# A hybrid decoder trunk on one core: two norms' reciprocals spread by split fp32r products, and conformer's variance computed in halves

## The chip, the cores and the metric

The kernel runs on one core of a Trainium2 chip. Five engines of the core work side by side, each through its own list of instructions in order: TensorE (PE in the profile, with its weight loads shown as PEld), VectorE (DVE), ScalarE (ACT), GpSimd (POOL) and SyncE (SP), which here only issues DMA. The metric is device time in microseconds of one execution, the median over several runs.

## The reference

One decoder layer on a sequence of 256 positions with 2048 features: an RMS norm, one wide input projection, sparse attention beside a causal conformer convolution, a shared output projection with a residual, a second RMS norm, a gated MLP with a short convolution, and a last RMS norm. The change touches the layer norm inside the conformer and the second RMS norm:

```python
def rms_norm(x, g):
    xf = x.astype(jnp.float32)
    y = xf * lax.rsqrt(jnp.mean(xf * xf, axis=-1, keepdims=True) + NORM_EPS)
    return (y * g.astype(jnp.float32)).astype(x.dtype)

def layer_norm(x, g, b):
    xf = x.astype(jnp.float32)
    mu = jnp.mean(xf, axis=-1, keepdims=True)
    xc = xf - mu
    var = jnp.mean(xc * xc, axis=-1, keepdims=True)
    y = xc * lax.rsqrt(var + NORM_EPS) * g.astype(jnp.float32) + b.astype(jnp.float32)
    return y.astype(x.dtype)
...
    u = layer_norm(u, ln_g, ln_b)
    return jax.nn.silu(u)
...
        x = x + jnp.concatenate([attn, conv], axis=-1) @ w_out[l]
        h = rms_norm(x, ffn_norm_g[l])
        x = x + conv_glu_ffn(h, w_up[l], ffn_conv_w[l], ffn_conv_b[l], w_down[l])
```

## The kernel before, in words

**Layout.** Activations lie feature by feature: 128 features on the partitions, 256 positions along the row. The weights come as tiles of 128x2048 fp32 (`wraw`, 1 MB each) over SyncE's queue. Each is split in two fp32r parts: ScalarE writes the high part `wh` (L126), VectorE or GpSimd the rest `wl = wraw - wh` (L131). The activations are split in the same way. A product is then three or so fast fp32r products with the high and low parts, summed in PSUM: the main stream is L454/L456 in the input projection, L189 to L191 in the output projection, L1188/L1190 in the MLP's first projection. Tiles are split two ahead of their use, out of three buffers.

**Order.** TensorE's list is written by hand. Between the products of a tile a `hook` (L428) runs at fixed places: it takes one step each from the lists `conf` (the conformer) and `steps`, and so many ticks of the attention (`attn_tick`, L980) as a table says. A tick does a slice of each of several stages (scores, smallest value, exponential, transposes, values) of different heads. The values of a head pair (`st_out`, L955) are products of 64 weight columns each, two halves `r` in turn, into the two halves of PSUM bank 7 (L966, L969). The last values' group is in the last tick, in the third tile of the output projection.

**Spreading a per-position number.** Both norms need one factor for each position in every partition. The sum over the features arrives with the positions on the partitions. GpSimd raises it to the power -0.5, VectorE multiplies the identity matrix `ident` by that column, which makes a 128x128 diagonal for each half `t` of the positions, and a product with a matrix of `ones` as weights writes that diagonal's values into all partitions. In the conformer that is `conf_var` (L578, the sum of the squares into two columns of bank 6), `conf_rstd` (L599), `conf_diag` (L606) and `conf_spread` (L584, then ScalarE copies the bank to `ck`), one per hook, started by `conf_norm` (L633) when the output projection's tile n = 2 begins. In the second norm it is `x2_rstd` (L1090) for each `t` and `x2_spread` (L1094) into bank 4, then a copy to `rB`; `x2_spread` is put by the table `between` (L1172) behind product pair 8 of the second half of the MLP's first tile, while the last feature blocks are still being transposed and split ahead of it (L1058, L225, L226). `rB` is applied only when the MLP's first results are taken out of PSUM, so TensorE's main stream does not wait for it.

`ones` and the diagonals are fp32 here, so these products run as fp32 products, and TensorE's list takes two passes for each.

Of the kernel before, what the change touches and what calls it, by code (L numbers as in the profile page):

```python
# [11 lines left out]
F32 = mybir.dt.float32  # L12
F32R = mybir.dt.float32r
AF = mybir.ActivationFunctionType
OP = mybir.AluOpType
PSUM = bass.MemoryType.PSUM

P = 128
T = 256
# [31 lines left out]
def hybrid_trunk(ctx: ExitStack, tc: tile.TileContext, a: dict, out: bass.AP):  # L51
    nc = tc.nc
# [148 lines left out]

    ident = consts.tile([P, P], F32, name="ident")
    make_identity(nc, ident)
    ones = consts.tile([P, P], F32, name="ones")
    nc.vector.memset(ones, 1.0)
    half = consts.tile([P, 1], F32, name="half")
    nc.vector.memset(half, -0.5)
# [10 lines left out]
    def rstd_of(pool, parts_, count, acc=EPS):  # L218

        r = pool.tile([P, 1], F32, name="rstd", bufs=2)  # L220
        nc.gpsimd.tensor_tensor(r, mean_of(pool, parts_, count, acc), half, op=OP.pow)
        return r

    def norm_evac(src, k, g):
        nc.scalar.activation(xt_h[:, k], src, AF.Copy, scale=g[:, k:k + 1])  # L225
# [11 lines left out]
    with ExitStack() as mx:  # L237
# [340 lines left out]
        def conf_var():  # L578
            cf["b"] = bank[6][:, :T]
            for t in range(2):  # L580
                nc.tensor.matmul(cf["b"][:, t:t + 1], cf["s"][:, 0, t * P:(t + 1) * P], ones[:, :1],
                                 start=True, stop=True)

        def conf_spread():  # L584
            nc.tensor.matmul(cf["b"], ones, cf["d"].rearrange("p t c -> p (t c)"), start=True, stop=True)
            conf_keep()

        def conf_apply(op, j0, n=2):
# [15 lines left out]
            cf["r"] = rv  # L604

        def conf_diag():  # L606
            cf["d"] = wk.tile([P, 2, P], F32, name="dg", tag="sg")
            for t in range(2):
                nc.vector.tensor_scalar_mul(cf["d"][:, t], ident, cf["r"][:, t:t + 1])

        def conf_swish(j0):
            for j in range(j0, j0 + 4):
# [19 lines left out]

        def conf_norm():  # L633
            conf.extend((
                no, no, conf_var, no, conf_rstd, no, conf_diag, no, conf_spread, no,
                *[lambda j=j: conf_apply(OP.mult, j) for j in (0, 2, 4, 6)],
                lambda: conf_swish(0), lambda: conf_swish(4), lambda: conf_split(0), lambda: conf_split(4)))

# [248 lines left out]


        TR_BANKS = (3, 6)
        units = [(i, r, br) for i in range(8) for r in range(2) for br in range(2)]  # L890
        US = {}

# [62 lines left out]
        def st_out(n):  # L955
            i = n // 4
            if n % 4 < 3:
                return
            o, q, m = bank[7], i // 4, i // 2
            assert cbst["done"] > m  # L960
            kw = dict(skip_group_check=True)
            for br in range(2):
                es = [US.pop(4 * i + 2 * r + br) for r in range(2)]
                for b, cols in enumerate((slice(0, T), slice(P, T))):
                    for r in range(2):
                        nc.tensor.matmul(o[64 * r:64 * r + 64, cols], vt[:, b, br, q, r],  # L966
                                         es[r][:, :T] if b == 0 else es[r][:, T:], start=br + b == 0, stop=False, **kw)
            for r in range(2):
                nc.tensor.matmul(o[64 * r:64 * r + 64, :T], vc[:, i % 2, q, r], cm["t"][:, m], start=False, stop=True,  # L969
                                 **kw)  # L970
            nc.scalar.activation(ma_h[:, i], o[:, :T], AF.Copy)
            nc.vector.tensor_sub(ma_l[:, i], o[:, :T], ma_h[:, i].bitcast(F32))
# [89 lines left out]
            norm_evac(x2_at(k), k, ffn_g)  # L1062

        for n, (qr, g) in enumerate(OUT_ORDER):
            if n == 1:
                assert tick["n"] > NU - 2
            if n == 2:
                x2 = mixp.tile([P, 2, D], F32, name="x2")
                nc.scalar.dma_start(ffn_g, a["vecs"][:, :KD])
                for t in range(2):  # L1070
                    nc.scalar.dma_start(x2[:, t], x_rows[:, t])
            if n == 2:
                conf_norm()
            if n == 3:
                assert tick["n"] == NU + DEEP
                st["lag"] = False
            if n == 8:
                step(count=99)
            ws = w_next(2)
            for t in range(2):  # L1080
                out_part(n, ws, qr, g, t)
                if g == 3:
                    steps.append(lambda qr=qr, t=t: out_resid(qr, t))
            if g == 3 and qr < 3:
                steps.extend([lambda: None] * 2 + [lambda qr=qr: (x2_tr(qr, 0), x2_tr(qr, 1))]
                             + [lambda k=k: (x2_evac(k), x2_evac(k + 1)) for k in range(4 * qr, 4 * qr + 4, 2)])
        acc = [mean_of(mixp, [ss2[:, t, i:i + 1] for i in range(3)], D) for t in range(2)]
        step(count=99)
        dg = mixp.tile([P, 2, P], F32, name="dg2")
        def x2_rstd(t):  # L1090
            r2 = rstd_of(mixp, [ss2[:, t, 3:4]], D, acc[t])
            nc.vector.tensor_scalar_mul(dg[:, t], ident, r2)

        def x2_spread():  # L1094

            for t in range(2):
                nc.tensor.matmul(bank[4][:, t * P:(t + 1) * P], ones, dg[:, t], start=True, stop=True)
            nc.scalar.activation(rB, bank[4][:, :T], AF.Copy)


    with ExitStack() as fx:
# [65 lines left out]
                    stages.remove(q)  # L1167


        for t in range(2):  # L1170
            x2_rstd(t)
        between = {(0, 6): lambda: (x2_tr(3, 0), x2_tr(3, 1)),  # L1172
# [207 lines left out]
```

## Time and profile before

| | |
|---|---|
| median of 3 runs | 1095.48 us (1095.45 to 1095.52) |
| the profiled execution's own time | 1095.29 us |
| its span, first to last instruction | 1093.5 us |
| granted TensorE clock, mean | 0.998 |
| TensorE busy | 1084.9 us, 99% |
| VectorE busy | 791.0 us, 72% |
| ScalarE busy | 602.2 us, 55% |
| GpSimd busy | 186.8 us, 17% |

The span lies inside the execution's time; what is around it (1.79 us) is start and end. A group row names line, engine, operation, what is written and read, the shape and the count, then busy time and mean ns. The chain of waits is followed back from the last instruction, and lists in order of time what the end depended on, with start and length in microseconds; on TensorE its lengths are the steps from one product to the next, while the durations in a timeline are modelled and overlap. In a timeline the bracket is the idle time ahead of an instruction and what ended it.

### The profile page before, as it was taken

How to read it: one execution, taken by the hardware profiler on the slowest of the kernel's cores; microseconds unless marked ns; L12 is line 12 of the kernel's file. 1: busy time of each engine (PE TensorE's matmuls, PEld its weight loads, DVE VectorE, ACT ScalarE, POOL GpSimd, SP SyncE). 2: the span in 40 equal slices, each digit the busy share in tenths (PEclk: the TensorE clock that was granted, in tenths of full speed). 3: DMA queues.
4: the chain of work that ended last, by engine and by line, in shares of the span. 5: the costliest groups of instructions: out<-in, count | busy, mean ns of one | idle time of the engine just before them, and what ended most of it. 6: DMA issues, size and time to landing. Idle time of an engine off the chain costs nothing.

```text
span 1093.5 us, 16270 instructions
## 1 busy us (share of the span) xinstructions
PE 1084.9 (99%) x6418; PEld 947.6 (87%) x6418; DVE 791.0 (72%) x1318; ACT 602.2 (55%) x915; POOL 186.8 (17%) x139
## 2 busy tenths in 40 slices
PE   9999999999999999999999999999999999999997
PEld 9888899887788888888888888888888888888886
DVE  7799989875656677777777777777777655665675
ACT  7644667887645555555555555545555544544552
POOL 0898775766000000000000000000000000000000
PEclk9999999999999999999999999999999999999999
DMA  9677535323654655555555555555554555556642
GB/s 363 241 265 261 178 127 174 116 78 138 248 193 166 237 186 192 191 190 192 193 192 193 193 188 186 187 186 186 189 191 151 193 188 189 198 179 203 232 161 77
DMA packets 34216, 207.55 MB, mean 190 GB/s; under 512 B 3883, under 2 KB 6715, under 8 KB 14428
## 3 DMA queue, kind: packets, MB, share of 16 engines
q1 hardware_dynamic: 30620, 199.46, 51.8%
q10 hardware_dynamic: 3520, 7.06, 1.8%
q8 instruction: 50, 0.82, 0.3%
q14 instruction: 26, 0.21, 0.1%
HBM read 204.39 MB, written 2.12 MB: 189 GB/s over the span
## 4 chain that ended last, share of the span: by engine, by line
PE 96%; DVE 2%; ACT 1%; issue 1%; POOLq 0%; POOL 0%; DVEq 0%; ACTq 0%
PE bank L1188 30%; PE bank L1207 17%; PE bank L1190 15%; PE bank L454 9%; PE bank L456 5%; PE bank L189 3%; PE bank L191 3%; PE bank L190 3%; PE bank L198 1%; PE bank L196 1%; PE bank L966 1%; PE bank L197 1%; PE bank L199 1%; PE bank L947 1%; PE bank L167 1%
## 5 line engine op out<-in xcount | busy, mean ns | idle before, releaser
L126 ACT ACTIVATE wh<-wraw 128x1024 fp32r<-128x1024 f32 (+3 forms) x248 | 355.8, 1452 | 344.5 <-issue 136.6
L131 DVE TENSOR_TENSOR wl<-wraw,wh 128x2048 fp32r<-128x2048 f32 (+2 forms) x194 | 361.7, 1873 | 206.1 <-ACT wh L126 206.1
L1188 PE MATMUL bank<-xt,wh 128*128 128x512 f32 x1408 | 488.5, 394 | 0.0
L1190 PE MATMUL bank<-xt,wl 128*128 128x256 f32 x1408 | 390.1, 277 | 0.0
L1188 PEld LDWEIGHTS bank<-xt,wh 128*128 128x128 f32 x1408 | 264.0, 188 | 61.2
L1190 PEld LDWEIGHTS bank<-xt,wl 128*128 128x128 f32 x1408 | 264.4, 188 | 0.0
L454 PE MATMUL bank<-xt,wh 128*128 128x512 f32 x464 | 150.6, 395 | 0.0
L1244 POOL TENSOR_TENSOR rstd<-ss,half 128x1 f32<-128x1 f32 x2 | 1.1, 548 | 730.4 <-DVE ss L1241 730.4
L131 POOL TENSOR_TENSOR wl<-wraw,wh 128x1024 fp32r<-128x1024 f32 (+1 forms) x54 | 121.2, 2271 | 19.8 <-ACT wh L126 15.3
L456 PE MATMUL bank<-xt,wl 128*128 128x256 f32 x464 | 105.8, 280 | 0.0
L489 DVE SCALAR_TENSOR_TENSOR bank<-us,cw,bank 128x256 f32<-128x256 f32 x232 | 95.0, 481 | 4.2 <-ACT bank L484 3.5
L454 PEld LDWEIGHTS bank<-xt,wh 128*128 128x128 f32 x464 | 80.8, 188 | 12.8 <-issue 0.6
L456 PEld LDWEIGHTS bank<-xt,wl 128*128 128x128 f32 x464 | 83.5, 188 | 8.4
L1207 PE MATMUL bank<-wl,gh 128*128 128x512 f32 x352 | 89.9, 336 | 0.0
L1207 PE MATMUL bank<-wh,gl 128*128 128x512 f32 x352 | 89.8, 336 | 0.0
L1207 PE MATMUL bank<-wh,gh 128*128 128x512 f32 x352 | 89.8, 336 | 0.0
L1151 DVE SCALAR_TENSOR_TENSOR yt<-u,fcw,yt 128x255 f32<-128x255 f32 (+1 forms) x176 | 80.9, 480 | 3.1
L941 POOL TENSOR_SCALAR e<-e,lsum 128x128 f32<-128x128 f32 x64 | 59.2, 940 | 36.3 <-ACT qs L824 15.7
L1207 PEld LDWEIGHTS bank<-wl,gh 128*128 128x128 f32 x352 | 54.1, 188 | 7.0
L1207 PEld LDWEIGHTS bank<-wh,gl 128*128 128x128 f32 x352 | 54.1, 188 | 6.9
L1207 PEld LDWEIGHTS bank<-wh,gh 128*128 128x128 f32 x352 | 54.0, 188 | 6.9
L1147 ACT ACTIVATE yt<-u,fcw 128x256 f32<-128x256 f32 x88 | 47.4, 586 | 0.0
(222 smaller groups left out, 1237.8 us busy)
## 6 DMA issues: line engine op xcount, KB each, us to landing
wraw<-in_w_u SPq DMA_DIRECT2D x88, 1024.0 KB, 4.8
wraw<-in_w_d SPq DMA_DIRECT2D x44, 768.0 KB, 4.2
wraw<-in_w_t SPq DMA_DIRECT2D x29, 1024.0 KB, 5.0
wraw<-in_w_o SPq DMA_DIRECT2D x16, 1024.0 KB, 5.0
wraw<-in_w_dl SPq DMA_DIRECT2D x11, 1024.0 KB, 4.8
wraw<-in_w_vg SPq DMA_DIRECT2D x4, 608.0 KB, 4.5
hb<-in_head SPq DMA_DIRECT2D x2, 1024.0 KB, 10.9
xr<-in_x SPq DMA_DIRECT2D x2, 1024.0 KB, 19.0
```

Of the source, the lines that this page charges most:

```text
L126: nc.scalar.activation(h[:, sl], raw[:, sl], AF.Copy)
L131: (nc.gpsimd if pooled else nc.vector).tensor_sub(l[:, sl], raw[:, sl], h[:, sl].bitcast(F32))
L189: nc.tensor.matmul(ps, xh, wh, start=first, stop=False)
L454: nc.tensor.matmul(ps, wh[:, sl], xt[:, kt].rearrange("p a t -> p (a t)"), start=kt == 0, stop=False)
L456: nc.tensor.matmul(ps[:, T:], wl[:, sl], xt_h[:, kt], start=False, stop=kt == KD - 1)
L489: nc.vector.scalar_tensor_tensor(y[:, j] if last else acc[0], us[:, j, k:k + T], cw[:, j, k:k + 1], acc[0], op0=OP.mult, op1=OP.add)
L941: nc.gpsimd.tensor_scalar_mul(e[:, lo:hi], e[:, lo:hi], lsum[:, br, t:t + 1])
L1147: nc.scalar.activation(yt, us_[i], AF.Identity, scale=fcw[:, c, 2:3], bias=fcw[:, c, 3:4])
L1151: nc.vector.scalar_tensor_tensor(ys[i][:, d:], us_[i][:, :T - d], fcw[:, c, k:k + 1], ys[i][:, d:], op0=OP.mult, op1=OP.add)
L1188: nc.tensor.matmul(bk[i], wh[:, k, sl], xt[:, kt].rearrange("p a t -> p (a t)"), start=kt == 0, stop=False)
L1190: nc.tensor.matmul(bk[i][:, T:], wl[:, k, sl], xt_h[:, kt], start=False, stop=kt == KD - 1)
L1207: nc.tensor.matmul(banks[n][:, :hi - lo], g[p][:, kt % 4, sl], ws[w][:, k * DW + lo:k * DW + hi], start=kt + i == 0, stop=i == 2 and kt == ...
```

## The change

Three things are changed.

1. `ones` becomes an fp32r tile (`ones_r`), with an fp32 view of the same bytes for all its other uses.
2. The diagonals of both norms are written in two fp32r parts by `diag_split`: the high part `identity * r`, and the rest `identity * r - high`. The spread is then two fp32r products of 256 columns with `ones_r`, summed in PSUM: in place of one fp32 product of 256 columns in the conformer, and of two with 128 in the second norm. The second norm's two tiles `dg2_h` and `dg2_l` lie in the MLP's pool `fp`, which takes over the memory of the pools of the mixer; `dg2` lay in `mixp`, the pool that lasts for the whole kernel.
3. `conf_var` makes its two products as four with 64 weight columns each, and is taken out of the conformer's list: it is put into the list `beside` when tile n = 2 begins, and `st_out` runs it ahead of the values of a whole group. The place is the last values' group.

```diff
-    ones = consts.tile([P, P], F32, name="ones")
+    ones_r = consts.tile([P, P], F32R, name="ones")
+    ones = ones_r.bitcast(F32)
...
+    def diag_split(d, t, r):
+        nc.vector.tensor_scalar_mul(d[0][:, t], ident, r)
+        nc.vector.scalar_tensor_tensor(d[1][:, t], ident, r, d[0][:, t].bitcast(F32), op0=OP.mult, op1=OP.subtract)
...
         def conf_var():
             cf["b"] = bank[6][:, :T]
             for t in range(2):
-                nc.tensor.matmul(cf["b"][:, t:t + 1], cf["s"][:, 0, t * P:(t + 1) * P], ones[:, :1],
-                                 start=True, stop=True)
+                for h in range(0, P, 64):
+                    nc.tensor.matmul(cf["b"][h:h + 64, t:t + 1], cf["s"][:, 0, t * P + h:t * P + h + 64], ones[:, :1],
+                                     start=True, stop=True)
 
         def conf_spread():
-            nc.tensor.matmul(cf["b"], ones, cf["d"].rearrange("p t c -> p (t c)"), start=True, stop=True)
+            for n, d in enumerate(cf["d"]):
+                nc.tensor.matmul(cf["b"], ones_r, d.rearrange("p t c -> p (t c)"), start=n == 0, stop=n == 1)
             conf_keep()
...
         def conf_diag():
-            cf["d"] = wk.tile([P, 2, P], F32, name="dg", tag="sg")
+            cf["d"] = [wk.tile([P, 2, P], F32R, name=nm, tag="sg") for nm in ("dg_h", "dg_l")]
             for t in range(2):
-                nc.vector.tensor_scalar_mul(cf["d"][:, t], ident, cf["r"][:, t:t + 1])
+                diag_split(cf["d"], t, cf["r"][:, t:t + 1])
...
-                no, no, conf_var, no, conf_rstd, no, conf_diag, no, conf_spread, no,
+                no, no, no, no, conf_rstd, no, conf_diag, no, conf_spread, no,
...
+        beside = []
...
             if n % 4 < 3:
                 return
+            while beside:
+                beside.pop(0)()
...
         for n, (qr, g) in enumerate(OUT_ORDER):
+            if n == 2:
+                beside.append(conf_var)
...
-        dg = mixp.tile([P, 2, P], F32, name="dg2")
         def x2_rstd(t):
             r2 = rstd_of(mixp, [ss2[:, t, 3:4]], D, acc[t])
-            nc.vector.tensor_scalar_mul(dg[:, t], ident, r2)
+            diag_split(dg, t, r2)
 
         def x2_spread():
 
-            for t in range(2):
-                nc.tensor.matmul(bank[4][:, t * P:(t + 1) * P], ones, dg[:, t], start=True, stop=True)
+            for n, d in enumerate(dg):
+                nc.tensor.matmul(bank[4][:, :T], ones_r, d.rearrange("p t c -> p (t c)"), start=n == 0, stop=n == 1)
             nc.scalar.activation(rB, bank[4][:, :T], AF.Copy)
...
+        dg = [fp.tile([P, 2, P], F32R, name=nm) for nm in ("dg2_h", "dg2_l")]
         for t in range(2):
             x2_rstd(t)
```

The order of instructions moves in three places. On TensorE, before, around conformer's variance in the third tile of the output projection (banks are numbered from 64 here, so bank_70 is bank 6 and bank_71 bank 7; `s` holds the folded squares, a shape is weight columns by columns):

```order
L581 MATMUL bank_70<-ones,s_2018 128x1 x2
L189 MATMUL bank_67<-wh,ma_h 128x512
L190 MATMUL bank_67<-wl,ma_h 128x512
L191 MATMUL bank_67<-wh,ma_l 128x512
L189 MATMUL bank_67<-wh,ma_h 128x512
L190 MATMUL bank_67<-wl,ma_h 128x512
L191 MATMUL bank_67<-wh,ma_l 128x512
L966 MATMUL bank_71<-es,vt 64x256 x2
L966 MATMUL bank_71<-es,vt 64x128 x2
```

And on TensorE after, at the same place (L587, L976 are the changed kernel's lines of the variance and the values):

```order
L189 MATMUL bank_67<-wh,ma_h 128x512
L190 MATMUL bank_67<-wl,ma_h 128x512
L191 MATMUL bank_67<-wh,ma_l 128x512
L587 MATMUL bank_70<-ones,s_2018 64x1 x4
L976 MATMUL bank_71<-es,vt 64x256 x2
L976 MATMUL bank_71<-es,vt 64x128 x2
```

The variance has moved behind six products of the main stream, and stands directly ahead of the values, with 64 weight columns as they have.

On VectorE, before, the diagonals of the second norm, at the start of the MLP, with the semaphores that an instruction waits for (`ms` is the mean of squares, `rstd` the reciprocal root, `dg_3710` the tile `dg2`, `x_3126` the residual stream):

```order
L1049 TENSOR_TENSOR x_3126<-bank_71,x_3126 128x512 [waits PE_49]
L214 TENSOR_SCALAR ms<-ss_2865,ms 128x1 [waits Activation_49]
L1092 TENSOR_SCALAR dg_3710<-ident,rstd 128x128 [waits Pool_49]
L214 TENSOR_SCALAR ms<-ss_2865,ms 128x1 [waits Activation_49]
L1092 TENSOR_SCALAR dg_3710<-ident,rstd 128x128 [waits Pool_49]
L226 SCALAR_TENSOR_TENSOR xt<-bank_64,ffn_g,xt 128x256 [waits Activation_49]
```

And after, where `dg_h` and `dg_l` are the two tiles' parts, and L231 is the old L226:

```order
L1059 TENSOR_TENSOR x_3126<-bank_71,x_3126 128x512 [waits PE_49]
L215 TENSOR_SCALAR ms<-ss_2865,ms 128x1 [waits Activation_49]
L226 TENSOR_SCALAR dg_h<-ident,rstd 128x128 [waits Activation_49,Pool_49]
L227 SCALAR_TENSOR_TENSOR dg_l<-ident,rstd,dg_h 128x128 [waits DVE_49]
L215 TENSOR_SCALAR ms<-ss_2865,ms 128x1
L226 TENSOR_SCALAR dg_h<-ident,rstd 128x128 [waits Pool_49]
L227 SCALAR_TENSOR_TENSOR dg_l<-ident,rstd,dg_h 128x128 [waits DVE_49]
L231 SCALAR_TENSOR_TENSOR xt<-bank_64,ffn_g,xt 128x256 [waits Activation_49]
```

Two operations are added, each waiting for the one ahead of it; the first diagonal now has ScalarE's semaphore as well, and the second mean comes behind the first pair. In the conformer VectorE's list changes in the same way, L609 twice becoming L226, L227, L226, L227, and nothing else moves there.

On TensorE after, the second norm's spread (bank_68 is bank 4; L1200 and L1202 are the old L1188 and L1190):

```order
L1200 MATMUL bank_66<-xt,wh 128x512 [waits DVE_49]
L1202 MATMUL bank_66<-xt,wl 128x256
L1108 MATMUL bank_68<-dg_h,ones 128x256 [waits DMAHW6_49,DMAHW2_49,PE_49]
L1108 MATMUL bank_68<-dg_l,ones 128x256
L1200 MATMUL bank_67<-xt,wh 128x512
```

Before, there was one row in their place, `L1097 MATMUL bank_68<-dg_3710,ones 128x128 x2`, without a wait. The lists of ScalarE, GpSimd and SyncE are the same in both kernels.

## The prediction

> **What bounds the kernel now.** I read the page's shares first, then TensorE's waits, then the chain of waits at the three places that the change touches, and last the timelines of VectorE there.
>
> The page, engines and chain:
>
> ```profile
> span 1093.5 us, 16270 instructions
> PE 1084.9 (99%) x6418; PEld 947.6 (87%) x6418; DVE 791.0 (72%) x1318; ACT 602.2 (55%) x915; POOL 186.8 (17%) x139
> PE 96%; DVE 2%; ACT 1%; issue 1%; POOLq 0%; POOL 0%; DVEq 0%; ACTq 0%
> ```
>
> TensorE's waits, the whole list:
>
> ```profile
> PE bank L279 <- DVE half L207: 1.0, 1, 1.0
> PE bank L905 <- DVE mn L915: 0.3, 1, 0.3
> ```
>
> A busy share says little where ends are modelled, but the chain lies on TensorE for 96%, and it stood for another engine twice in all, both before the change's places. So at the change's places a microsecond less on TensorE is a microsecond less in the end, until another engine comes late. How much TensorE time is at stake stands in the chain (start, length in us). Conformer's variance and the group of values, then the first spread:
>
> ```profile
> 272.03 0.23 PE bank L191
> 272.27 0.34 PE bank L581 x4
> 272.61 0.34 PE bank L189
> 272.94 0.23 PE bank L190
> ...
> 274.11 1.45 PE bank L966 x16
> 275.56 0.43 PE bank L969 x4
> 275.99 0.43 PE bank L189
> 276.42 0.23 PE bank L190
> ...
> 282.95 0.24 PE bank L191
> 283.19 0.43 PE bank L585 x2
> 283.62 0.23 PE bank L189
> ```
>
> and the second norm's spread:
>
> ```profile
> 361.95 0.23 PE bank L1188
> 362.18 0.12 PE bank L1190
> 362.30 0.45 PE bank L1097 x4
> 362.75 0.23 PE bank L1188
> ```
>
> The x counts show that an fp32 product is two passes: two variance products are x4, one spread is x2. A 512-column product of the main stream takes 0.23, a 256-column one in fp32r (L1190) 0.12. So the variance costs 0.34 plus the 0.11 that the L189 behind it takes over its usual 0.23: **0.45**. The spreads cost **0.43** and **0.45**. All that the change can take away is therefore 1.33 us, 0.12% of the span; about 0.2% (2.2 us) is what a measurement of this kernel can tell from no change.
>
> **The spreads.** Before, 256 columns took two fp32 passes of 0.43 / 2 = 0.215 each; after, two fp32r products of 256 columns at L1190's 0.12 each, so 0.24. Each needs a weight load of its own; L1190 needs one too, and its 0.12 holds it. First spread: 0.43 - 0.24 = 0.19. Second: 0.45 - 0.24 = 0.21. Bounds: L1190's 0.12 is the same type and width, so I see no way below 0.24; above, a product that ran at the fp32 pass of 0.215 would give nothing back.
>
> **The variance.** Two products with 128 weight columns become four with 64, at the head of the values' group. Weight loads there and in the variance (group rows: count, busy, mean ns), and the first loads and products of the values within a stretch that ends at 274.05:
>
> ```profile
> L966 PEld LDWEIGHTS bank<-es,vt 128*64 128x64 f32 x16 | 1.0, 136 | 0.7 <-issue 0.4
> L581 PEld LDWEIGHTS bank<-ones,s 128*128 128x128 f32 x4 | 0.6, 190 | 0.1
> ```
>
> ```profile
> 274.04 0.14 PEld L966 LDWEIGHTS bank<-es,vt 128*64 128x64 f32 x2 [0.37 <-issue]
> ...
> L966 PE MATMUL bank<-es,vt x2: 430/430/431, 274.0 to 274.0; 128*64 128x256 f32 x2
> ```
>
> Four passes of one column in 0.45 are 0.112 each, and one column is no work: what is paid is the load of 128 weight columns. A load of 64 columns is 190 - 136 = 54 ns shorter, so about 0.058. And halves run beside each other: L969's four passes of 256 columns with 64 weight columns take 0.43, as L585's two with 128 do, and the first two loads and products of the values start within 0.01 us (274.04 to 274.05). The variance's halves alternate as the values' do, so eight passes are four pairs: 4 x 0.058 = **0.23**. The turn to 64-column weights and back is paid by the values already (0.20 on the L189 behind them); conformer's halves come in front of them and behind the turn. Gain 0.45 - 0.23 = 0.22. Bounds: 0 if all of it vanished under the turn (gain 0.45); 0.46 if the halves went one after the other (loss 0.01); 0.90 if each of eight passes took the 0.112 of a full load (loss 0.45). I take the pairs, since L969 is the nearest row. The Trainium skill's page "TensorEngine Tiling (Array Packing)", section Instruction Overhead, speaks against the halves: about 60 cycles for each matmul however few its columns, and no tiling of a dimension that is already small. By that rule the eight passes would be some 0.20 us, an estimate at the 2.4 GHz of that skill's page "TensorE: Matmul & The Clock Gate", and the sum below would be 0.03 larger; the trace's 0.112 for a one-column pass says that here the load sets the price.
>
> **Later variance, its reader.** The products move from 272.3 to about 274.1. Their only reader is VectorE's L601, behind L972 and three splits:
>
> ```profile
> 276.45 0.42 DVE L972 TENSOR_TENSOR ma_l<-bank,ma_h 128x256 fp32r<-128x256 f32 x1 [6.80 <-ACT ma_h L971]
> 276.80 3.49 DVE L131 TENSOR_TENSOR wl<-wraw,wh 128x1024 fp32r<-128x1024 f32 x3
> 280.20 0.15 DVE L601 TENSOR_SCALAR rv<-bank 128x2 f32<-128x2 f32 x1
> 281.04 0.29 DVE L609 TENSOR_SCALAR dg<-ident,rv 128x128 f32<-128x128 f32 x1 [0.69 <-POOL rv L603]
> 281.56 0.29 DVE L609 TENSOR_SCALAR dg<-ident,rv 128x128 f32<-128x128 f32 x1 [0.23 <-POOL rv L603]
> 281.76 2.36 DVE L131 TENSOR_TENSOR wl<-wraw,wh 128x1024 fp32r<-128x1024 f32 x2
> ```
>
> It comes at 280.20, 5 us behind: nothing. L972 waits for the values, which now end 0.22 earlier, so this line moves as TensorE does.
>
> **The split diagonals.** Two more VectorE operations at each place, 128x128. The row below does the same at 256 columns, so each is at most 479 ns; L609's 290 is the floor:
>
> ```profile
> L226 DVE SCALAR_TENSOR_TENSOR xt<-bank,ffn_g,xt 128x256 fp32r<-128x256 f32 x16 | 7.0, 479 | 6.6 <-ACT xt L225 6.4
> ```
>
> First norm: the diagonals end at 281.56 + 0.29 = 281.85, the spread starts at 283.19 and its weight load one 0.24 product earlier, at 282.95. Cover 1.1 us against at most 0.96, of which 0.23 falls into the idle time in front of the second L609. Nothing; without cover, up to 0.96. The splits of weights behind it slip by under 0.8 us; TensorE waits for no wl in the whole trace, and the list above is all its waits. Second norm:
>
> ```profile
> 355.27 0.19 ACT L1050 ACTIVATION_READ_ACCUMULATOR sq<-x 128x1 f32 x1
> ```
>
> ```profile
> 355.42 0.29 DVE L1092 TENSOR_SCALAR dg<-ident,rstd 128x128 f32<-128x128 f32 x1 [0.66 <-POOL rstd L221]
> 355.62 0.21 DVE L214 TENSOR_SCALAR ms<-ss,ms 128x1 f32<-128x1 f32 x1
> 356.49 0.29 DVE L1092 TENSOR_SCALAR dg<-ident,rstd 128x128 f32<-128x128 f32 x1 [0.66 <-POOL rstd L221]
> ...
> 357.89 0.88 DVE L226 SCALAR_TENSOR_TENSOR xt<-bank,ffn_g,xt 128x256 fp32r<-128x256 f32 x2
> 359.23 2.36 DVE L131 TENSOR_TENSOR wl<-wraw,wh 128x1024 fp32r<-128x1024 f32 x2 [0.46 <-ACT wh L126]
> ```
>
> The new first diagonal also waits for ScalarE's sum (355.27 + 0.19, so 0.04 to 0.2 us later, in place of the L214 behind it), and the first split pushes L214, GpSimd's second power and all that follows. Together 0.2 + 2 x 0.48 = 1.2 us at most. The second diagonal's pair then ends near 358, the spread is at 362.30: 4 us of cover. The evacuations queued behind (L226, last at 358.8) end by 360, and TensorE reads their first block only in the product ahead of the spread, at 361.95; the split at 359.23 had 0.46 idle ahead of it. Nothing.
>
> **A new wait.** The second spread's first product now waits for two DMA semaphores and TensorE's own. In the built program the counts asked for are reached by loads at the kernel's start and by the output projection's last product, near 352. Nothing. Had the count been that of gfin's load:
>
> ```profile
> L1108 ACTq DMA_DIRECT2D gfin<-in_final_g x1: 455/455/455, 355.8 to 355.8; - x1
> ...
> DMA to landing us min/median/max: 5.0/5.0/5.0
> ```
>
> it lands at 360.8, still 1.5 us ahead.
>
> **Sum.** 0.19 + 0.21 + 0.22 = 0.62 us less. Against the profiled execution's span: 1093.5 - 0.62 = 1092.9; its time of 1095.29 has 1.79 around the span and lies 0.19 under the median of 1095.48. That median less 0.62 is **1094.86**.
>
> **The rivals.** *The halves do not pair.* For it: one column gives no time in which the other half's load could hide, and sixteen short instructions follow each other closer than anywhere in the trace. Against it: L969. One after the other: 0.40 - 0.01 = 0.39 less, 1095.09; at 0.112 each, 0.40 - 0.45, 1095.53. The Trainium skill's "TensorE: Matmul & The Clock Gate", section Back-to-back issue gap, has a case in which each matmul costs about 62 ns of issue; by it eight would be 0.50 (an estimate) and the end 1095.13, though the two products within 0.01 us above contradict it.
>
> *The change does not do what it says:* fp32r products with ones as weights run at fp32's pace, and the spreads give nothing. For: the trace has no fp32r product with these weights. Against: L1190. Then only 0.22 is won: 1095.26.
>
> *Slower: the splits hold up conformer's spread.* A DVE write of the low part that costs as a split of 128x1024 does (3.49 / 3 = 1.16) would add 2.3 - 0.23 = 2.1 us to a cover of 1.1; TensorE stands 1.0 us, net +0.4: 1095.9. It decides from 0.67 us for each of the two added operations, is slower than before from 0.98, and over 0.2% slower only from 2.1 us. Against: 479 ns at twice the width.
>
> **How the numbers follow.** Forecast 0.68; halves unpaired 0.15; spreads without gain 0.06; splits late 0.05; something else, either way, 0.06. Range: the low end is the forecast with a variance that costs nothing, 1095.48 - 0.85 = 1094.6, less 0.2 by which one execution lay under the median: 1094.4. The high end takes in both cases of smaller gain, 1095.53, rounded to 1095.6. Left out are the late splits and half of the rest, about 0.08. Every case named lies within 2.2 us of 1095.48, so the 0.2% bound is passed only by something unnamed: faster 0.03, within 0.94, slower 0.03.
>
> **What would show it.** Right: on the chain, the spreads at about 0.24 for x2 each, the variance at about 0.23 for x8 directly ahead of the values, the L189 in its old place at 0.23, L601 straight behind the splits with no idle time, and no new row in TensorE's waits. Wrong: a row of x8 at 0.4 or more (unpaired), a spread near 0.43 (no gain), or a wait of TensorE for dg_l or for a DMA at either spread.

## The result and the profile after

| | before | after |
|---|---|---|
| median of six runs each | 1095.43 us (1095.29 to 1095.52) | 1103.93 us (1103.81 to 1104.17) |
| span of the profiled execution | 1093.5 us | 1102.2 us |
| granted TensorE clock, mean | 0.998 | 0.998 |

The ratio is 1.0078, with a 95% interval of 1.0068 to 1.0088: the change makes the kernel 8.5 us slower. The forecast was 0.6 us faster, and its range ended at 1095.6. Beside the first four experiments one of before's 25 executions took 5019 us; it stands in no comparison.

The page of after, engines and the chain's shares by engine:

```profile
span 1102.2 us, 16279 instructions
PE 1093.6 (99%) x6420; PEld 951.3 (86%) x6420; DVE 792.3 (72%) x1322; ACT 602.5 (55%) x915; POOL 187.0 (17%) x139
PE 97%; DVE 1%; issue 1%; ACT 1%; POOLq 0%; POOL 0%; ACTq 0%
```

TensorE's busy time grew by 8.7 us for two instructions more; that of VectorE, ScalarE and GpSimd by 1.3 us or less. The list of its waits in after is still two lines:

```profile
PE bank L284 <- DVE half L208: 1.0, 1, 1.0
PE bank L913 <- DVE mn L923: 0.3, 1, 0.3
```

So TensorE is not kept waiting. The chain of waits of after at the three places (start, length in us), first around the variance:

```profile
267.42 0.23 PE bank L189
...
273.56 0.23 PE bank L191
273.79 0.33 PE bank L587 x8
274.12 1.36 PE bank L976 x16
275.48 0.43 PE bank L979 x4
275.91 0.43 PE bank L189
...
283.11 0.23 PE bank L592 x2
283.34 0.24 PE bank L189
...
362.03 0.24 PE bank L1108 x2
362.27 0.23 PE bank L1200
```

This is what was forecast. The spreads take 0.23 and 0.24 for x2. The variance takes 0.33 for x8, but the values behind it only 1.36 in place of 1.45, since the step to 64-column weights is now paid ahead of them: 0.33 - 0.09 = 0.24. Against before, the product behind the second spread starts at 362.27 and not at 362.75, 0.48 us earlier, although this execution was 0.12 us late before the first of the three places. There the same L189 starts at 267.42 in after, and in before's chain at:

```profile
267.30 0.23 PE bank L189
```

Up to here, then, the change has won 0.60 us. The 8.7 us by which the span is longer are lost behind the second spread, and what had been won with them. The loss can be dated with a table by stage. Its columns are the window, the sum, and the busy time and count of each engine, then the granted clock, DMA share and GB/s. The MLP's first projection runs from 352 us to 842 in before and to 850 in after, and the down projection follows. Before:

```profile
300.00:360.00 60.00, 60.00 (x285) 49.26 (x284) 37.88 (x56) 31.35 (x52) 1.09 (x2) 1.00 0.54 195
400.00:600.00 200.00, 200.00 (x1156) 174.89 (x1155) 147.46 (x198) 102.24 (x128) 0.00 (x0) 1.00 0.54 190
620.00:840.00 220.00, 220.00 (x1271) 192.37 (x1271) 163.04 (x220) 114.30 (x142) 0.00 (x0) 1.00 0.53 187
860.00:1060.00 200.00, 200.00 (x1156) 177.32 (x1155) 122.20 (x88) 100.98 (x89) 0.00 (x0) 1.00 0.56 194
```

And after:

```profile
300.00:360.00 60.00, 60.00 (x285) 49.31 (x284) 37.75 (x57) 30.61 (x52) 1.10 (x2) 1.00 0.53 196
400.00:600.00 200.00, 200.00 (x1134) 173.41 (x1133) 145.10 (x194) 100.56 (x126) 0.00 (x0) 1.00 0.53 187
620.00:840.00 220.00, 220.00 (x1247) 190.91 (x1246) 160.60 (x214) 110.65 (x137) 0.00 (x0) 1.00 0.52 184
860.00:1060.00 200.00, 200.00 (x1155) 177.33 (x1154) 122.20 (x89) 100.02 (x88) 0.00 (x0) 1.00 0.58 196
```

Read the first count of each row: TensorE's products. Ahead of the spread (300 to 360) and in the down projection (860 to 1060) both kernels make the same number, but for one. In the first projection after makes 1134 where before makes 1156, and 1247 where it makes 1271: 1.9% fewer in each window, so evenly over the whole stage. The granted clock is 1.00 in all rows, the busy share full. VectorE, ScalarE and the DMAs do a little less in the same time, as TensorE does.

The main stream there is a pair for each feature block and weight tile: a product of 512 columns (L1188, in after L1200) and one of 256 (L1190, in after L1202). Four pairs of it in the chain of before (two in the middle left out):

```profile
499.92 0.12 PE bank L1190
500.03 0.23 PE bank L1188
500.26 0.11 PE bank L1190
500.38 0.23 PE bank L1188
...
501.07 0.23 PE bank L1188
501.30 0.12 PE bank L1190
```

and in that of after:

```profile
499.94 0.12 PE bank L1202
500.06 0.23 PE bank L1200
500.29 0.12 PE bank L1202
500.41 0.23 PE bank L1200
...
501.12 0.23 PE bank L1200
501.35 0.12 PE bank L1202
```

From the first to the last row four pairs take 1.38 us before and 1.41 after. Two decimals are too coarse for a difference of 2%, so here are the steps from one product's start to the next, in ns, from the same traces (512 columns, 256 columns, and so on):

```
before  233 117 231 113 | 232 118 231 112 | 233 117 231 113            two pairs repeat
after   232 118 240 120 236 114 | 232 118 240 120 236 113              three pairs repeat
```

Each is a steady rhythm: its mean over any 34 us between 364 and 840 us is 346.6 to 346.7 ns a pair before, 353.3 to 353.4 after. Below they are called the fast and the slow rhythm. The spread stands behind 25 of the stage's 1408 pairs; the 1383 others times 6.6 ns make 9.1 us. Less the 0.6 won before, that is the 8.5 measured. The slow rhythm begins within three pairs of the second spread (steps behind it: 229 114 232 118 241 120 235 114) and lasts to the stage's end.

### The profile page after: what moved, and what is told of

It reads as the page before. It is cut to its first block, busy times and chain, and to the rows that moved or that the text cites. A ratio compares the mean times of both kernels' runs of the same rounds, so it can differ in the third digit from the quotient of the medians.

```text
span 1102.2 us, 16279 instructions
## 1 busy us (share of the span) xinstructions
PE 1093.6 (99%) x6420; PEld 951.3 (86%) x6420; DVE 792.3 (72%) x1322; ACT 602.5 (55%) x915; POOL 187.0 (17%) x139
## 4 chain that ended last, share of the span: by engine, by line
PE 97%; DVE 1%; issue 1%; ACT 1%; POOLq 0%; POOL 0%; ACTq 0%
PE bank L1200 30%; PE bank L1219 17%; PE bank L1202 15%; PE bank L459 9%; PE bank L461 5%; PE bank L189 3%; PE bank L191 3%; PE bank L190 3%; PE bank L198 1%; PE bank L196 1%; PE bank L976 1%; PE bank L955 1%; PE bank L199 1%; PE bank L197 1%; PE bank L167 1%
## 5 line engine op out<-in xcount | busy, mean ns | idle before, releaser
L1200 PE MATMUL bank<-xt,wh 128*128 128x512 f32 x1408 | 497.6, 399 | 0.0
L1202 PE MATMUL bank<-xt,wl 128*128 128x256 f32 x1408 | 395.4, 281 | 0.0
L1200 PEld LDWEIGHTS bank<-xt,wh 128*128 128x128 f32 x1408 | 264.6, 188 | 65.8
L1202 PEld LDWEIGHTS bank<-xt,wl 128*128 128x128 f32 x1408 | 266.0, 189 | 0.0
L459 PE MATMUL bank<-xt,wh 128*128 128x512 f32 x464 | 150.6, 395 | 0.0
L461 PE MATMUL bank<-xt,wl 128*128 128x256 f32 x464 | 105.8, 280 | 0.0
```

Of the source, the lines that this page charges most:

```text
L459: nc.tensor.matmul(ps, wh[:, sl], xt[:, kt].rearrange("p a t -> p (a t)"), start=kt == 0, stop=False)
L461: nc.tensor.matmul(ps[:, T:], wl[:, sl], xt_h[:, kt], start=False, stop=kt == KD - 1)
L1200: nc.tensor.matmul(bk[i], wh[:, k, sl], xt[:, kt].rearrange("p a t -> p (a t)"), start=kt == 0, stop=False)
L1202: nc.tensor.matmul(bk[i][:, T:], wl[:, k, sl], xt_h[:, kt], start=False, stop=kt == KD - 1)
```

## The experiments

Three theories at first. **Rhythm**: the two narrow products of the spread, behind the stream's own narrow one, set the stream into another steady rhythm, and nothing else is wrong. **Memory**: the diagonals in the pool `fp` move its other tiles, and the stream reads or writes at worse addresses. **Waits**: the three semaphore waits that the spread's first product now has. Each median is given beside that of before, measured together with it.

**The conformer's part alone.** The second norm is as before (fp32 diagonal in `mixp`, two fp32 products of 128 columns); all else is the change.

> The changed kernel with its second norm as before (one fp32 diagonal in mixp, two fp32 products); conformer's part of the change stays. Theory 'rhythm' (the alternating 512/256-column stream of the MLP can run in two steady rhythms, 347 and 353 ns a pair, and the products that interrupt it last set which): the stream keeps 347, so 0.2 to 0.3 us under before, about 1095.2. Theory 'memory' (the MLP's pools moved by 1 KB a partition, and TensorE's reads meet other engines' there): also fast, about 1095.2, since dg2 is back in its place. Both say the loss is all in the second norm's part; if it stays at 1104, conformer's part is to blame and both fall.

Measured: 1094.92 us against 1095.35 (ratio 0.9996, 0.9987 to 1.0006). The loss is gone, so all of it belongs to the second norm. What is left agrees with 0.19 + 0.22 forecast for the conformer, though no interval here resolves 0.4 us.

**The place alone.** Before, with the fp32 diagonal in `fp`, in as much room as after takes:

```diff
-        dg = mixp.tile([P, 2, P], F32, name="dg2")
+        dg = fp.tile([P, 4, P], F32, name="dg2")[:, :2]
```

> The kernel before with nothing changed but the place of dg2: its room (twice the size, as in the changed kernel) is taken from the MLP's pool, so that pool's addresses and the new waits of the spread are those of the changed kernel; the spread stays two fp32 products. 'Rhythm': same as before, 1095.4. 'Memory', or a third theory that the waits do it: the whole loss, about 1104.

Measured: 1095.41 against 1095.35 (1.0001, 0.9991 to 1.0010). The tile's place brings the shifted addresses and the same waits at the spread. Neither costs anything by itself; that both theories fall is shown by the fourth run, which is slow with neither.

**One fp32 product behind the changed spread.** Its result is read by nobody.

```diff
+            nc.tensor.matmul(bank[4][:, T:T + P], ones, ident, start=True, stop=True)
```

> The changed kernel with one more product behind the second spread: ones times the identity in fp32, 128 columns, into the unused half of bank 4; its result is read by nobody. 'Rhythm': two fp32 passes set the stream back to 347 ns a pair, so the loss goes: 1095.4 - 0.5 + 0.2, about 1095.1. 'Memory' or waits: 1104.2, the loss stays and 0.2 is added.

Measured: 1095.00 against 1095.35 (0.9997, 0.9987 to 1.0007). A product more, and the kernel is 8.9 us faster than after.

**Two narrow fp32r products behind the spread of before**, read by nobody, with the stream's own tiles:

```diff
+            for _ in range(2):
+                nc.tensor.matmul(bank[4][:, T:], xt_h[:, 0, :P], xt_h[:, 0], start=True, stop=True)
```

> The kernel before with two more fp32r products of 256 columns behind its fp32 spread, with activations as weights, into the unused half of bank 4, read by nobody; no address, diagonal or wait differs from before. 'Rhythm', if it is the fp32r products of 256 columns that set the slow one: 353 ns a pair from there to the end of the MLP's first projection, about 1095.4 + 0.2 + 9.2 = 1104.8. 'Memory' or waits: 1095.7.

Measured: 1104.83 against 1095.35 (1.0087, 1.0071 to 1.0103). The loss is made in the kernel before, with no line of the change in it. The table by stage of this kernel shows after's counts:

```profile
400.00:600.00 200.00, 200.00 (x1134) 173.39 (x1133) 144.22 (x194) 101.18 (x126) 0.00 (x0) 1.00 0.53 189
```

So the rhythm stands. The next runs ask what about the two products does it: their **type**, the **run** of narrow products one behind the other, the **moment**, or their **sum** of time.

**The changed spread as four fp32r products of 128 columns.**

> The changed kernel with its second spread as four fp32r products of 128 columns instead of two of 256. That the rhythm of the MLP's stream is set at the spread stands by now; open is by what. Theory 'type' (leaving off on fp32r products keeps or brings the slow rhythm, fp32 passes bring the fast one): slow, about 1104.2. Theory 'run' (three 256-column products in a row, the stream's own and the spread's two, push the stream out): fast, about 1095.0 with products at 0.11 each. Theory 'moment' (any shift of the stream against something that runs on by itself): either.

Measured: 1095.03 against 1095.40 (0.9996, 0.9987 to 1.0006). The same type, weights and data, fast. But these products are not half as long as the two: in this run's chain the four take 0.40 us (L1109 x4), and the L1201 behind them 0.28 in place of 0.23, so 0.45 in all, what before's fp32 spread took. So this run does not part the type from the time. The runs below with one narrow product and with the two apart do: their products are fp32r with 256 columns, and they are fast.

**The changed spread one pair later** (behind pair 9 in place of 8).

> The changed kernel with its second spread one product pair later (behind pair 9 instead of 8). 'Type' and 'run': slow as before it, 1103.9. 'Moment', if it is the place among the pairs (the fast rhythm repeats every two pairs): fast, about 1094.9.

Measured: 1103.88 against 1095.40 (1.0077, 1.0062 to 1.0092). Behind either of the two neighbouring pairs the stream turns slow, though the pair directly ahead has other steps (232 118 ns in after, 231 115 here).

**Only one narrow product behind the spread of before.**

> The kernel before with one fp32r product of 256 columns behind its fp32 spread, where two gave 1104.8; its result is read by nobody. 'Type': slow, about 1104.7. 'Run': fast, 1095.5, since only one 256-column product stands ahead of the next 512.

Measured: 1095.48 against 1095.40 (1.0001, 0.9992 to 1.0010): fast.

**The changed spread as one product of 512 columns**, both parts side by side in bank 4; VectorE adds the two halves.

```diff
-            for n, d in enumerate(dg):
-                nc.tensor.matmul(bank[4][:, :T], ones_r, d.rearrange("p t c -> p (t c)"), start=n == 0, stop=n == 1)
+            nc.tensor.matmul(bank[4], ones_r, dg2.rearrange("p a t c -> p (a t c)"), start=True, stop=True)
             nc.scalar.activation(rB, bank[4][:, :T], AF.Copy)
+            nc.vector.tensor_add(rB, rB, bank[4][:, T:])
```

> The changed kernel with its second spread as one fp32r product of 512 columns (high and low diagonals side by side in one tile), and the two halves added by VectorE after ScalarE's copy. 'Type': slow, about 1103.9. 'Run': fast, about 1094.9, since a 512-column product keeps wide and narrow apart. VectorE's added 0.4 us lies beside TensorE's work in both.

Measured: median 1104.62 against 1095.40 (1.0084, 1.0067 to 1.0101). But of its five executions one took 1095.66 us and four 1104.51 to 1104.67, at granted clocks of 0.998 and 0.999: by its times one program takes either rhythm. The profiled one was the short one; of a long one there is no trace. In it the stream is fast from the spread on, and bank 4 adds a wait, since the stream needs that bank while VectorE's add is still queued behind a split of weights:

```profile
PE bank L1201 <- DVE rB L1109: 0.4, 1, 0.4
```

**The same single product into bank 1**, which the stream needs later.

> The changed kernel with its second spread as one fp32r product of 512 columns, as in the run that came out at both 1095.7 and 1104.6, but into bank 1, which TensorE needs only some 15 us later, so that it no longer stands 0.4 us for VectorE's sum. 'Run', with the stand as what set the rhythm anew: fast in every run, 1094.8. If the 512-column product itself leaves it open, both values again.

Measured: 1094.81 (1094.71 to 1095.18, eleven runs) against 1095.46 (0.9994, 0.9985 to 1.0003). Fast in every run, and the added wait is gone. So the long executions go with bank 4 and its wait; which of the two matters, no run parts.

**The two narrow products apart**: the high part behind pair 8, the low part behind pair 9, a stream pair between them.

```diff
-            for n, d in enumerate(dg):
-                nc.tensor.matmul(bank[4][:, :T], ones_r, d.rearrange("p t c -> p (t c)"), start=n == 0, stop=n == 1)
-            nc.scalar.activation(rB, bank[4][:, :T], AF.Copy)
+            n = spread.pop(0)
+            nc.tensor.matmul(bank[4][:, :T], ones_r, dg[n].rearrange("p t c -> p (t c)"), start=n == 0, stop=n == 1)
+            if n == 1:
+                nc.scalar.activation(rB, bank[4][:, :T], AF.Copy)
...
-                   (0, 8): lambda: (x2_evac(14), x2_evac(15), w_pump()), (1, 8): x2_spread}
+                   (0, 8): lambda: (x2_evac(14), x2_evac(15), w_pump()), (1, 8): x2_spread, (1, 9): x2_spread}
```

> The changed kernel with the two products of its second spread apart: the high diagonal's behind pair 8, the low one's behind pair 9. The same two fp32r products of 256 columns with the same operands and waits; only no three narrow products follow each other, but twice two. Theory 'run' (three 256-column products in a row push the stream into the slow rhythm): fast, 1095.4 - 0.6 = 1094.8, the whole of the change's local gain and none of its loss. Theory 'sum' (what counts is that two narrow products were put in between, wherever, since with one the stream stayed fast): slow, 1103.9.

Measured: 1094.75 (1094.55 to 1095.20, eleven runs) against 1095.46 (0.9994, 0.9985 to 1.0003). This is the whole change, in the time that was forecast for it (1094.86): 9.2 us under after. It is the lowest median of all kernels here, but its interval takes in 1, so it is not shown to beat before. Its table by stage has before's counts again:

```profile
400.00:600.00 200.00, 200.00 (x1156) 176.34 (x1155) 147.90 (x199) 102.07 (x127) 0.00 (x0) 1.00 0.54 190
```

**A third narrow product in the changed spread.**

> The changed kernel with a third fp32r product of 256 columns behind the second spread's two, read by nobody: four narrow products in a row. 'Run' in its plain form (three or more): slow, 1104.0. If slow and fast go by the exact number instead, as a shift of the stream in a pattern that repeats, it may be fast: 1094.9.

Measured: 1104.12 against 1095.46 (1.0079, 1.0064 to 1.0094): slow.

Up to here two or three narrow products together were slow, one, or two apart, fast. The remaining runs put disturbances far from the spread: in the first product loop of m = 11, behind pair 8: at 605 us in after, at 601 us in before. In after the stream is slow there, in before fast.

**After, with one fp32 product at m = 11** (`ones` and `ident`, read by nobody).

> The changed kernel with one fp32 product of ones and the identity, read by nobody, in the middle of the MLP's first projection (tile pair m = 11, behind pair 8 of its first half). If the rhythm holds itself up and an fp32 product resets it at any time, the stream is slow for 688 of the 1383 pairs behind the spread and fast for the rest: 1103.9 - 4.5 + 0.2 = 1099.6. If what slows it is lasting (memory, waits), 1104.1.

Measured: 1104.21 against 1095.46 (1.0080, 1.0066 to 1.0094). A miss: what kept the stream fast behind the spread does not bring it back from the slow rhythm.

**After, with eight fp32 transposes at m = 11**, the kind of work that stands ahead of the stream's fast stretch in all these kernels (L1058).

> The changed kernel with eight fp32 transposes of 128 columns, read by nobody, in the middle of the MLP's first projection (m = 11, behind pair 8). At the projection's start the stream is slow for its first six pairs in every kernel, and fast behind the eight transposes there. If such a stretch sets it fast at any time: slow for 688 of 1383 pairs, 1103.9 - 4.5 + 0.9 = 1100.3. If it depends on the moment: 1104.8.

Measured: 1100.23 (1100.04 to 1100.42) against 1095.35 (1.0045, 1.0028 to 1.0062). It comes back. The two windows of one execution, on either side of the transposes:

```profile
400.00:600.00 200.00, 200.00 (x1134) 173.53 (x1134) 145.06 (x194) 100.56 (x126) 0.00 (x0) 1.00 0.53 187
620.00:840.00 220.00, 220.00 (x1271) 193.98 (x1270) 163.70 (x220) 113.56 (x141) 0.00 (x0) 1.00 0.53 188
```

1134 is after's count, 1271 is before's. The chain of this kernel at the turn:

```profile
604.70 0.24 PE bank L1200
604.93 0.12 PE bank L1202
605.06 0.23 PE bank L1200
605.29 0.12 PE bank L1202
605.41 0.87 PE bank L1205 x8
606.28 0.23 PE bank L1200
```

The steps in ns ahead of them are 233 117 241 120 236 113, and from the third pair on 230 117 in every pair. (The slow pairs at the stage's start, of which the expectation counts six, are seven in the traces.)

**After, with one narrow product at m = 11.**

> The changed kernel with one fp32r product of 256 columns behind pair 8 at m = 11, read by nobody: does one narrow product shift the slow stream into the fast rhythm, as one or two apart left the fast one alone? If any shift sets the rhythm anew: 1103.9 - 4.5 + 0.1 = 1099.5. If the slow rhythm holds against small disturbances, as it held against one fp32 product: 1104.0.

Measured: 1104.00 against 1095.35 (1.0079, 1.0064 to 1.0094): the slow rhythm goes on.

**Before, with two narrow products together at m = 11** (bank 0).

> The kernel before, untouched at its norms, with two fp32r products of 256 columns together behind pair 8 at m = 11, read by nobody; with the stream's own that makes three narrow ones in a row. 'Run': slow from there on, 695 pairs at 6.6 ns, 1095.4 + 4.6 + 0.2 = 1100.2. If it is the place of the spread and what surrounds it: 1095.6.

Measured: 1095.58 against 1095.35 (1.0002, 0.9993 to 1.0011). A miss, and the important one: the run of three narrow products that turned the stream at 363 us does not turn it here. The run of narrow products as a general rule falls.

**Before, with two apart at m = 11.**

> As the run with two narrow products together at m = 11, but one behind pair 8 and one behind pair 9. 'Run': fast throughout, 1095.4 + 0.2 = 1095.6. 'Moment': 1100.2 as well.

Measured: 1095.51 against 1095.35 (1.0002, 0.9992 to 1.0011): fast, which after the last result tells little.

Between the spread and m = 11 more differed than the moment: the bank that the products write and the place in the tile, which two more runs change, and two things that no run changes. In after the two products are `ones` times diagonals and the first has semaphore waits, while here they are activations; and where the same activations turned the stream, at 363 us in before, four fp32 passes stood directly ahead of them.

**After, with its spread into bank 1**, nothing else changed.

> The changed kernel with the same two 256-column products at the same place, written to bank 1 in place of bank 4. If what counts is the two narrow products together at this moment, whatever they write to: 1103.9 us as after, the pair at 353 ns. If the bank that they write decides (bank 4 is the one that the main stream takes next): the fast rhythm, about 1094.8 us.

Measured: 1104.07 against 1095.34 (1.0080, 1.0063 to 1.0097). Not the bank.

**Before, with two narrow products at m = 10**, into bank 4, behind pair 8 of the second half, with the stream in banks 2 and 3: as at the spread, 222 us later.

> The kernel before with two 256-column fp32r products that nobody reads, written to bank 4 behind the same pair of the tile as the spread (second half, pair 8), but at m = 10, where the stream works in the same banks 2 and 3 as at the spread. If bank and place in the tile decide (the earlier two products at m = 11 went to bank 0, in the first half): slow for the 743 pairs that follow, 743 x 6.6 ns = 4.9 us and 0.2 for the products, 1100.5 us. If the moment behind the transposes decides: 1095.6 us.

Measured: 1095.54 against 1095.34 (1.0002, 0.9992 to 1.0011). Its row behind that place has before's count:

```profile
620.00:840.00 220.00, 220.00 (x1271) 192.33 (x1270) 163.15 (x221) 114.12 (x142) 0.00 (x0) 1.00 0.53 187
```

Neither bank nor place in the tile decides, then. The rhythm ahead does not either: the steps in ns directly ahead of the two products are 231 113 232 118 in after at 362 us, and the same four in before's run at 601 us; in after the next steps are 121 116 229, here 119 117 233. What is left is the moment, or what goes with it: the products' operands and waits in after, the fp32 passes ahead of them in before.

The stream itself differs in one thing as well, which no run touched. Near the spread its own 512-column products still wait for a semaphore at every second pair, as the feature blocks have just been written (in after the weight loads at 361.41, 362.34 and 363.04 us carry such a wait, which costs no time that the profile shows); near the later products it carries none (between 581.29 and 586.96 us around the two at 584.41, between 598.24 and 603.91 around the two at 601.36).

**Shown**, by the two directions (taken out: the conformer alone, the product behind, the parts apart; put in: two narrow products in before): the loss is the slow rhythm of the main stream, entered at the second spread because two 256-column products stand together there. Memory, waits, the type and the bank are excluded as the cause by themselves, and the granted clock is the same. **Open** stays the rule: why two such products turn the stream at 363 us and not at 584 or 601 us, and why the single 512-column product goes either way in bank 4. What the moment at 363 us has of its own is only argued: beside the waits just named, the last transposes end some six microseconds earlier (in before at 355.18 + 0.87). Two narrow products shortly behind transposes at a later m were not tried, nor after's own two products at a later m, nor the two of activations at 363 us without the fp32 passes ahead.

## Why the prediction was wrong

**The spreads.** 0.43 to 0.24 and 0.45 to 0.24 were forecast; the chain shows 0.23 and 0.24. Right, to a hundredth.

**The variance.** 0.23 as four pairs was forecast; 0.24 net. In the trace the two products of a pair start 5 to 7 ns apart, and from the second pair on they follow each other in 58 ns. The loads pair, and the rival of unpaired halves falls.

**The later variance, its reader.** Nothing, as forecast. VectorE's line in after, the reader (now L608) right behind the splits, no idle time ahead of it:

```profile
276.71 3.49 DVE L131 TENSOR_TENSOR wl<-wraw,wh 128x1024 fp32r<-128x1024 f32 x3
280.12 0.15 DVE L608 TENSOR_SCALAR rv<-bank 128x2 f32<-128x2 f32 x1
```

**The split diagonals.** Forecast: at most 0.48 us each, covered. VectorE in after, conformer and second norm:

```profile
281.28 0.35 DVE L227 SCALAR_TENSOR_TENSOR dg_l<-ident,rv,dg_h 128x128 fp32r<-128x128 f32 x1
281.55 0.28 DVE L226 TENSOR_SCALAR dg_h<-ident,rv 128x128 fp32r<-128x128 f32 x1
281.87 0.35 DVE L227 SCALAR_TENSOR_TENSOR dg_l<-ident,rv,dg_h 128x128 fp32r<-128x128 f32 x1
...
355.29 0.29 DVE L226 TENSOR_SCALAR dg_h<-ident,rstd 128x128 fp32r<-128x128 f32 x1 [0.80 <-ACT sq L1060]
...
357.07 0.35 DVE L227 SCALAR_TENSOR_TENSOR dg_l<-ident,rstd,dg_h 128x128 fp32r<-128x128 f32 x1
```

0.35 each; ready at 282.22 for a spread at 283.11, and at 357.42 for one at 362.03. The rival of late splits falls. The new waits cost nothing either: the run with the place alone has them.

**The step that failed** is the premise that carried all of these to the end: "at the change's places a microsecond less on TensorE is a microsecond less in the end, until another engine comes late". Nobody came late. The main stream itself, untouched by the diff, went on at another pace behind the spread: 353.3 ns a pair in place of 346.7, 1383 times. The sum counted each new product's own duration and took its neighbours' as given; a term of 9.1 us was missing beside one of 0.21. L1190's 0.12 was the right price for the product, but a price read in one rhythm says nothing of what the product does to that rhythm. No rival held it, and "something unnamed" on the slower side had 0.03. What turns the rhythm is shown above only in part.

A sign was there. The same two lines run at both paces in the trace of before: the stage's first seven pairs, ahead of the last transposes, stand in its chain between these two rows:

```profile
352.71 0.23 PE bank L1188
...
355.18 0.87 PE bank L1058 x8
```

2.47 us for seven pairs are 353 ns a pair; at 500 us it is 1.38 / 4 = 345 (346.7 by the finer steps). Single rows of 0.23 and 0.12 hide that; sums over several pairs, or the number of products in equal windows, show it.

The Trainium skill's page "TensorE: Matmul & The Clock Gate", section Back-to-back issue gap, says that in a stream of weight loads and products the spacing is set by both, pipelined, and not by the columns alone. The trace agrees that it is no constant of the width: a 512-column step takes 230 to 241 ns here, by rhythm and position. That page of the Trainium skill gives one sustained figure for 512 columns, about 131 ns, which no 512-column step here comes near, and it does not say that one stream has two spacings at the same granted clock.

## What to carry to other kernels

A product put between those of a steady stream has two prices: its own time, and what the stream's pace becomes behind it. The second can be many times the first, so compare products per window (or pairs per microsecond) well behind every place that a change touches, before and after, even where no wait and no clock has changed. Where the pace has shifted, try the same work in another grouping: here the parts one stream pair apart, or one wide product into a bank that the stream needs later, were worth 9 us.

## What the runs showed of the hardware that was not expected

- A stream of alternating 512- and 256-column fp32r products, each with its own weight load, has more than one steady rhythm at a granted clock of 1.00. Two forms share 346.7 ns a pair (steps 233 117 231 113, and 230 117); one takes 353.3 (232 118 241 120 236 113). Each holds for hundreds of pairs.
- A disturbance can move the stream from one to the other, both ways: into the slow one by two narrow products at 363 us, out of it by eight transposes at 605 us. One fp32 product or one narrow product did not move it out, and two narrow products of activations at 584 or 601 us did not move it in.
- By its times the same program can take either: the 512-column spread in bank 4, where TensorE waits 0.4 us for that bank, ran at 1095.66 us once and at 1104.5 to 1104.7 four times; in bank 1, without the wait, at 1094.7 to 1095.2 eleven times.
- A narrower fp32r product with its own weight load need not be shorter: four of 128 columns took 0.45 us, two of 256 columns 0.24.
- Eight one-column fp32 passes with 64 weight columns take 0.24 us, as four pairs of about 0.06; four passes with 128 weight columns took 0.45.
